# Stores issued behind the loads of the sixth later pair instead of the fourth, in a batched matrix product

## The chip, the cores and the metric

The kernel runs on one core of a Trainium2 chip. The metric is the device time of one execution in microseconds (us). "Span" is the time from the first to the last instruction in a trace; it is about 1.8 us less than the device time of the same execution. Each transfer that uses all 16 DMA engines of the core shows 16 completions in the trace; it has "landed" with the last of them. The engines work through their own queues of transfers ("rings"). "Granted clock" is the share of TensorE's full clock that the profile shows.

## The reference

```python
b1, b2, m, k, n = 8, 16, 256, 512, 384        # 128 products of (256 x 512) by (512 x 384), float32
def reference(x, weight):
    return np.matmul(x, weight).astype(np.float32)
```

## The kernel before

The 128 products are taken in 64 pairs, 0 to 63. For each pair SP (SyncE) issues one load of x (1 MB), two of w (768 KB each) and one store (768 KB). DVE casts to bf16, PE transposes x and multiplies, ACT copies the product out of PSUM, the memory that PE writes to. Each engine has its own program, and they meet at semaphores. The parts that matter (cuts marked):

```python
    AHEAD = 4
    XS, WS, OS = AHEAD, AHEAD * G, 8        # buffers of x, of w, of the product; G = 2
    # ...
    def load(e, n, n0):
        wait(e, x_cast, n - XS + 1)         # the cast of pair n-4 has freed the x buffer
        e.dma_start(x_sb[n0 % XS][:], ...).then_inc(x_in[n0 % XS], 16)
        for i in range(G):
            wait(e, w_cast, n * G + (i + 1 - WS))
            e.dma_start(w_sb[(n0 * G + i) % WS][:], ...).then_inc(w_in[(n0 * G + i) % WS], 16)

    def store(e, n, n0):
        e.wait_ge(o_copied, n * G + G)      # ACT has copied pair n out
        e.dma_start(out=o_rows[...], in_=out_sb[n0 % OS][:]).then_inc(o_out[n0 % OS], 16)
    # ...
    @block.sync
    def _(e):
        U = OS
        for n in range(AHEAD):
            load(e, n, n)
        rounds = (NG - AHEAD) // U
        with e.Fori(0, rounds) as t:
            for s in range(U):
                load(e, t * U + (AHEAD + s), AHEAD + s)
                store(e, t * U + s, s)
        for n in range(rounds * U, NG):
            if n + AHEAD < NG:
                load(e, n + AHEAD, n + AHEAD)
            store(e, n, n)
        # ... then wait for all stores
```

## Time and profile before

| | kernel before |
|---|---|
| device time, median of 3 (range) | 524.96 us (524.79 to 526.66) |
| span of the profiled execution | 524.6 us |
| moved by DMA | 218.12 MB, 414 to 426 GB/s in all of the 40 slices but the first and the last |
| busy share PE, DVE, ACT | 65%, 52%, 39% |

Read it from the transfers: 64 pairs move the same bytes whatever the order, and no compute engine comes near its limit. Only the first and the last of the 40 slices (335 and 238 GB/s) lie far below the steady rate of about 424.

### The profile page before, as it was taken

How to read it: one execution, taken by the hardware profiler on the slowest of the kernel's cores; microseconds unless marked ns; L12 is line 12 of the kernel's file. 1: busy time of each engine (PE TensorE's matmuls, PEld its weight loads, DVE VectorE, ACT ScalarE, POOL GpSimd, SP SyncE). 2: the span in 40 equal slices, each digit the busy share in tenths (PEclk: the TensorE clock that was granted, in tenths of full speed). 3: DMA queues.
4: the chain of work that ended last, by engine and by line, in shares of the span. 5: the costliest groups of instructions: out<-in, count | busy, mean ns of one | idle time of the engine just before them, and what ended most of it. 6: DMA issues, size and time to landing. Idle time of an engine off the chain costs nothing.

```text
span 524.6 us, 5588 instructions
## 1 busy us (share of the span) xinstructions
PE 338.9 (65%) x1536; PEld 191.9 (37%) x1536; DVE 272.4 (52%) x320; ACT 204.3 (39%) x257; POOL 0.7 (0%) x6
## 2 busy tenths in 40 slices
PE   3755676756747576675776656666657666766764
PEld 2533333333333343343333333333334333433331
DVE  4655454464554554645545446455454464554641
ACT  1652424344333343342433434444334334344242
POOL 0000000000000000000000000000000000000000
PEclk9997868688787877878778778787787878778686
DMA  8999999999999999999999999999999999999995
GB/s 335 421 415 414 422 420 424 424 424 421 424 423 423 424 423 424 425 420 425 423 423 424 420 423 426 421 424 425 422 425 422 424 424 422 424 424 422 426 423 238
DMA packets 36868, 218.16 MB, mean 416 GB/s; under 512 B 4096, under 2 KB 4096, under 8 KB 28672
## 3 DMA queue, kind: packets, MB, share of 16 engines
q1 hardware_dynamic: 36864, 218.12, 99.9%
q14 instruction: 3, 0.02, 0.0%
q8 instruction: 1, 0.02, 0.0%
HBM read 167.77 MB, written 50.33 MB: 416 GB/s over the span
## 4 chain that ended last, share of the span: by engine, by line
SPq 73%; DMA 15%; issue 7%; PE 2%; DVE 1%; ACTq 0%; DVEq 0%; ACT 0%
SPq L101 47%; DMA w_sb<-in_weight_dram 15%; SPq L110 14%; SPq L95 10%; PE po L163 2%; SPq L90 1%; DVE x_t L133 1%; DVE w_bf L124 0%; SPq L109 0%; ACTq _compat.py:109 0%; SPq L201 0%; PE pt L151 0%; DVEq L90 0%; DVEq L131 0%; ACT out_sb L180 0%
## 5 line engine op out<-in xcount | busy, mean ns | idle before, releaser
L180 ACT COPY out_sb<-po 64x768 f32<-64x768 f32 x256 | 203.0, 793 | 314.4 <-PE po L163 311.7
L163 PE MATMUL po<-w_bf,x_t 128*128 128x384 bf16 x1024 | 251.9, 419 | 95.3 <-DVE x_t L133 95.3
L163 PEld LDWEIGHTS po<-w_bf,x_t 128*128 128x128 bf16 x1024 | 119.4, 122 | 216.6 <-issue 182.0
L119 DVE CAST x_bf<-x_sb 128x2048 bf16<-128x2048 f32 x64 | 78.5, 1227 | 200.0 <-DMA x_sb<-in_x_dram 200.0
L124 DVE CAST w_bf<-w_sb 128x1536 bf16<-128x1536 f32 x128 | 122.3, 955 | 40.2 <-DMA w_sb<-in_weight_dram 40.2
L151 PE MATMUL pt<-identity,x_bf 128*128 128x128 f32 x512 | 87.7, 322 | 83.8 <-DVE x_bf L119 83.5
L151 PEld LDWEIGHTS pt<-identity,x_bf 128*128 128x128 f32 x512 | 72.5, 211 | 109.1 <-issue 107.9
L133 DVE COPY x_t<-pt 128x1024 bf16<-128x1024 bf16 x128 | 82.2, 683 | 1.1 <-PE pt L151 1.1
L180 ACT ACT_TABLE_LOAD x1 | 1.3, 1283 | 0.9 <-SPq L48 0.9
masks.py:199 POOL TENSOR_SCALAR_AFFINE_SELECT identity<-identity 128x128 f32<-128x128 f32 x1 | 0.3, 293 | 0.2 <-POOL identity L190 0.2
L190 POOL MEMSET identity<- 128x128 f32 x1 | 0.2, 204 | 0.5 <-SPq L48 0.5
L253 POOL MEMSET const-bfloat16-1.0<- 128x1 bf16 x1 | 0.1, 101 | 0.0
L253 POOL MEMSET const-uint8-127<- 128x1 uint8 x1 | 0.1, 101 | 0.0
L253 POOL MEMSET const-float32-0.0<- 128x1 f32 x1 | 0.1, 98 | 0.2 <-issue 0.2
L253 POOL MEMSET const-float32-1.0<- 128x1 f32 x1 | 0.1, 98 | 0.0
## 6 DMA issues: line engine op xcount, KB each, us to landing
w_sb<-in_weight_dram SPq DMA_DIRECT2D x128, 768.0 KB, 22.3
x_sb<-in_x_dram SPq DMA_DIRECT2D x64, 1024.0 KB, 22.6
out_dram<-out_sb SPq DMA_DIRECT2D x64, 768.0 KB, 21.7
```

Of the source, the lines that this page charges most:

```text
L90: e.wait_ge(sem, value)
L95: e.dma_start(x_sb[n0 % XS][:], x_rows[bass.ds(n * (G * M), G * M)].rearrange("(p r) k -> p r k", r=R),).then_inc(x_in[n0 % XS], 16)
L101: e.dma_start(w_sb[(n0 * G + i) % WS][:], w_rows[bass.ds(n * (G * K) + i * K, K)].rearrange("(p ko) n -> p ko n", ko=KO),).then_inc(w_in[( ...
L110: e.dma_start(out=o_rows[bass.ds(n * (G * M), G * M)].rearrange("(p r) n -> p r n", r=R), in_=out_sb[n0 % OS][:],).then_inc(o_out[n0 % OS] ...
L119: e.tensor_copy(out=x_bf[n0 % BS][:], in_=x_sb[n0 % XS][:]).then_inc(x_cast, 1)
L124: e.tensor_copy(out=w_bf[(n0 * G + i) % WBS][:], in_=w_sb[(n0 * G + i) % WS][:]).then_inc(w_cast, 1)
L133: e.tensor_copy(out=x_t[n0 % TS][:, j, :, :, g : g + 2].rearrange("k h i g c e -> k g (h i) (c e)"), in_=pt[(n0 * T + q) % PT][:].bitcast( ...
L151: ins = e.transpose(pt[(n0 * T + q) % PT][:, rr, h, :], words[:, 2 * q + rr, h :: KO // 2], identity[:],)
L163: ins = e.matmul(po[(n0 * G + i) % PO][:, j, :N], x_t[n0 % TS][:, j, ko // 2, i, :, :, ko % 2].rearrange("k g c -> k (g c)"), w_bf[(n0 * G ...
L180: ins = e.copy(out=out_sb[n0 % OS][i * C : (i + 1) * C, g::G, :], in_=po[(n0 * G + i) % PO][g * C : (g + 1) * C, :, :N],)
L190: e.memset(identity[:], 0.0).then_inc(id_done, 1)
L253: nc = _bacc.Bacc("TRN2", target_bir_lowering=False, num_devices=1)
```

## The change

The intent is to let loads run further ahead of stores, so that a store, and the wait that it brings to the issuing queue, never holds a load back, and so that more stores are left to fill the queue while the last pair is computed. All the change is on SP:

```diff
+    LAG = 6
 ...
-        for n in range(AHEAD):
+        for n in range(LAG):
             load(e, n, n)
-        rounds = (NG - AHEAD) // U
+        rounds = (NG - LAG) // U
         with e.Fori(0, rounds) as t:
             for s in range(U):
-                load(e, t * U + (AHEAD + s), AHEAD + s)
+                load(e, t * U + (LAG + s), LAG + s)
                 store(e, t * U + s, s)
         for n in range(rounds * U, NG):
-            if n + AHEAD < NG:
-                load(e, n + AHEAD, n + AHEAD)
+            if n + LAG < NG:
+                load(e, n + LAG, n + LAG)
             store(e, n, n)
```

The buffers stay as they are: four of x, eight of w, eight of the product.

## The prediction

> **What bounds the kernel now.** I read the page first, parts 2 to 4, then the windows of the last microseconds, then the store's line in small windows, then the timeline, then the waits of the issuing queue.
>
> The page, part 2, 40 slices of 13.1 us each:
>
> ```profile
> DMA  8999999999999999999999999999999999999995
> GB/s 335 421 415 414 422 420 424 424 424 421 424 423 423 424 423 424 425 420 425 423 423 424 420 423 426 421 424 425 422 425 422 424 424 422 424 424 422 426 423 238
> ...
> q1 hardware_dynamic: 36864, 218.12, 99.9%
> ```
>
> The transfers bound it. They run at 420 to 426 GB/s in all slices but the first (335) and the last (238), while the busiest compute engine, PE, is at 65%. A change that moves no fewer bytes can only win in those two slices. The first loses its time before any transfer starts (4 GB/s in the window of 0 to 2 us), and every load in it is the same in both kernels. What remains is the last slice. Windows of one microsecond there (columns: window, length, busy us and count of PE, PEld, DVE, ACT, POOL, granted clock, DMA share, GB/s):
>
> ```profile
> 515.00:516.00 1.00, 1.00 (x5) 0.50 (x4) 0.00 (x0) 0.12 (x1) 0.00 (x0) 0.50 1.03 430
> 516.00:517.00 1.00, 1.00 (x5) 0.50 (x4) 0.00 (x0) 0.99 (x2) 0.00 (x0) 0.50 0.77 320
> 517.00:518.00 1.00, 1.00 (x5) 0.32 (x3) 0.00 (x0) 0.48 (x1) 0.00 (x0) 0.76 0.15 61
> 518.00:519.00 1.00, 0.01 (x1) 0.00 (x0) 0.00 (x0) 0.94 (x2) 0.00 (x0) 1.00 0.06 25
> 519.00:520.00 1.00, 0.00 (x0) 0.00 (x0) 0.00 (x0) 0.64 (x1) 0.00 (x0) 1.00 0.03 12
> 520.00:521.00 1.00, 0.00 (x0) 0.00 (x0) 0.00 (x0) 0.00 (x0) 0.00 (x0) 0.95 0.56 233
> 521.00:522.00 1.00, 0.00 (x0) 0.00 (x0) 0.00 (x0) 0.00 (x0) 0.00 (x0) 0.50 1.03 424
> 522.00:523.00 1.00, 0.00 (x0) 0.00 (x0) 0.00 (x0) 0.00 (x0) 0.00 (x0) 0.50 0.33 129
> ```
>
> The hole from about 516.8 to 520.4 is the prize: most DMA engines have nothing to do until the last pair's product is copied out (ACT ends at 519.6) and its store, the only one left, runs from 520.4. But the share in the hole is not zero: 0.15, then 0.06. One sixteenth is 0.0625, so one engine of the 16 is still at work there at its usual rate: a straggler with a backlog.
>
> How late it is, the last five stores tell (answers for the store's line in small windows: start of the issue, and time to landing, which is when the last of the 16 engines is done):
>
> ```profile
> L110 SPq DMA_DIRECT2D out_dram<-out_sb x1: 1609/1609/1609, 492.6 to 492.6; - x1
> DMA to landing us min/median/max: 21.8/21.8/21.8
> L110 SPq DMA_DIRECT2D out_dram<-out_sb x1: 332/332/332, 503.1 to 503.1; - x1
> DMA to landing us min/median/max: 15.1/15.1/15.1
> L110 SPq DMA_DIRECT2D out_dram<-out_sb x1: 332/332/332, 509.8 to 509.8; - x1
> DMA to landing us min/median/max: 10.2/10.2/10.2
> L110 SPq DMA_DIRECT2D out_dram<-out_sb x1: 332/332/332, 519.7 to 519.7; - x1
> DMA to landing us min/median/max: 3.2/3.2/3.2
> ```
>
> Call the pairs 0 to 63. Store 59 lands at 492.6 + 21.8 = 514.4, store 61 at 518.2, store 62 at 520.0, store 63 at 522.9. From 59 to 62 they are (520.0 - 514.4) / 3 = 1.87 us apart: back to back on the slowest engine. Store 63 comes 2.9 us after 62, so this engine had a hole of only 2.9 - 1.87 = 1.0 us. The span ends 1.7 us after that landing (524.6).
>
> The timeline shows the rhythm, by the casts of x, which start when their load lands:
>
> ```profile
> 492.75 1.23 DVE L119 CAST x_bf<-x_sb 128x2048 bf16<-128x2048 f32 x1 [3.21 <-DMA x_sb<-in_x_dram]
> ...
> 500.81 1.23 DVE L119 CAST x_bf<-x_sb 128x2048 bf16<-128x2048 f32 x1 [3.21 <-DMA x_sb<-in_x_dram]
> ...
> 508.89 1.23 DVE L119 CAST x_bf<-x_sb 128x2048 bf16<-128x2048 f32 x1 [3.22 <-DMA x_sb<-in_x_dram]
> ```
>
> 8.07 us per pair, with DVE waiting 3.2 us for each. At the start, with loads alone in the queue, the same casts start at 5.88, 12.12, 18.36 and 24.61: 6.24 us per pair of loads. The difference, 1.83 us, is what one store costs among loads; the 1.87 of stores alone is nearly the same. So mixing loads and stores costs nothing that I can see, and re-ordering them should save nothing in the steady part.
>
> **What the Trainium skill says.** "HBM Reference", Specifications, gives about 425 GB/s for a core that streams alone, bounded by its 16 DMA engines; the trace agrees with 424. "DMA: Bandwidth & Descriptors", Queues, rings and completion order, says that each engine consumes descriptors in ring order and that one transfer is split over up to 16 rings; its section on why a DMA increments by 16 says these engines finish independently. The trace agrees: store 62 lands at 520.0 although total traffic collapses at about 516.8. The same page, Anatomy of one DMA, says semaphore waits happen on the issuing sequencer, not in the DMA engines; so what a load waits for depends on what was issued before it, and the order of issue is all that this diff changes.
>
> **The change, part by part.** No instruction on PE, DVE, ACT or POOL changes; the listing of both kernels differs there by line numbers only. On SP the same 192 loads and 64 stores are issued; six pairs of loads instead of four go before the first store. The buffers stay: four of x, eight of w, so load m still waits for the cast of pair m-4.
>
> 1. Start. Loads 4 and 5 come before store 0. Before, store 0 went out at 17.1 after a wait for ACT, and load 5 only behind it at 17.75. Load 5 can now go when cast 1 is over (13.4). But a transfer lands 22 us after its issue (median), so the queue is deep and stays fed either way. Gain: 0.
>
> 2. Steady part. The queue's own waits are short: the store's wait for ACT is 29.8 us in all, of which 25.6 us lie in the last 40 us, the loads' wait for DVE 10.9 us. SP otherwise stands in the issue instruction itself (1.3 to 5 us each), held by the full queue. So load m goes out about when pair m-3 lands, in both kernels. Moving stores back by two pairs exchanges places in a queue that never empties. Gain: 0. The out buffers have room: store n now goes out as pair n+3 lands and itself lands 22 us, or 2.7 pairs, later; its buffer is wanted for the copy of pair n+8, over 2 pairs after that.
>
> 3. Tail. Load 63 had stores 0 to 58 ahead of it, and now has 0 to 56. Two stores less are 2 x 1.87 = 3.7 us: the last x lands at 505.1 instead of 508.8, and the chain from there to the issue of store 63 (cast, transposes, copies, matmuls, ACT: 519.7 - 508.8 = 10.9 us) ends at about 516.0. That is the gain offered. But behind load 63 now stand six stores (57 to 62) instead of four. The straggling engine has the same bytes to move before store 63 in both kernels, so it is through at 520.0 in both. Store 63 is then already waiting, and lands 1.87 us later, at 521.9, instead of 522.9. Gain: the straggler's hole, 1.0 us, and no more.
>
> Sum: 0 + 0 - 1.0 to -1.1 us, thus 524.96 - 1.1 = 523.9 us, 0.2% less.
>
> **Rivals.** (a) *The full 3.7 us.* If the engines were level, the hole would be 3.5 us for all, and the shift would fill it: 521.3 us. For it: the fifteen other engines. Against it: the 0.06 of DMA share between 518 and 519, and the landing of store 62. A smaller spread in unprofiled runs doesn't open it either: then the last load lands earlier in the old kernel too, and its hole is the same. (b) *No gain.* The last matmuls ran at a granted clock of 0.50 (4.91 us; 2.77 us for an earlier pair at 1.00). In an execution where the clock happens to be full there, the old chain is about 2 us shorter and the old kernel has no hole on the straggler: 525.0 us. For it: the clock alternates all through the run. (c) *Slower, by a wait on the out buffers or by starving compute behind the first six loads.* A wait on the out buffers would need a store to take 40 us instead of 22. Loads alone come every 6.24 us, and DVE needs 272.4 / 64 = 4.3 us per pair, PE 338.9 / 64 = 5.3; at half clock PE needs 1.8 + 4.9 = 6.7, for a few pairs only. I would give it at most 526.
>
> **Range and chances.** Centre 523.9. Below, the full shift with less spread is unlikely, so 522.8. Above, rival (b) and the noise of the runs before (524.79 to 526.66) give 525.3. A change of 2% is 10.5 us; the two end slices together don't hold that much outside the bytes. Faster 0.01, same 0.98, slower 0.01.
>
> **What would show it.** In the new profile: slices 2 to 39 still near 424; the last slice up from 238 to about 285 GB/s (3.76 MB in 13.1 us, if the fifteen run through to about 519.2); the last matmuls starting near 509.4 instead of 513.1; store 63 issued near 516, landing some 6 us later instead of 3.2, and 1.9 us behind store 62; the store's wait for ACT in the tail well under 25.6 us. The prediction is wrong if store 62 lands much before 520 (the straggler depended on the order of transfers), or if the steady rhythm leaves 8.07 us per pair (mixing does cost), or if the first slices lose rate.

## The result, and the profile after

| | before | after |
|---|---|---|
| device time, median (range), 4 runs each | 525.28 us (524.79 to 526.66) | 525.24 us (524.97 to 525.32) |
| span of the profiled execution | 524.6 us | 523.4 us |

The ratio is 0.9994, with a 95% interval of 0.9974 to 1.0014: the same. Ratios here are the mean time of one kernel's fast runs over that of the other's fast runs of the same rounds, so they are not quite the ratios of the medians.

The changed kernel, page part 2, the 40 slices:

```profile
DMA  8999999999999999999999999999999999999996
GB/s 336 421 419 419 426 420 424 424 423 422 423 424 423 422 424 423 423 425 420 424 425 422 424 423 424 424 422 424 425 422 424 424 425 424 422 422 426 423 424 259
```

The first slice (336 for 335) and the steady ones are unchanged, but for the third and the fourth (419 each, for 415 and 414). The last went from 238 to 259. The windows of its end (same columns as in the prediction):

```profile
517.00:518.00 1.00, 0.00 (x0) 0.00 (x0) 0.00 (x0) 0.00 (x0) 0.00 (x0) 0.50 1.01 418
518.00:519.00 1.00, 0.00 (x0) 0.00 (x0) 0.00 (x0) 0.00 (x0) 0.00 (x0) 0.50 0.24 98
519.00:520.00 1.00, 0.00 (x0) 0.00 (x0) 0.00 (x0) 0.00 (x0) 0.00 (x0) 0.50 0.07 31
520.00:521.00 1.00, 0.00 (x0) 0.00 (x0) 0.00 (x0) 0.00 (x0) 0.00 (x0) 0.50 0.06 25
521.00:522.00 1.00, 0.00 (x0) 0.00 (x0) 0.00 (x0) 0.00 (x0) 0.00 (x0) 0.50 0.02 6
```

Before, the hole came ahead of the last store, for most engines. Now there is no hole ahead of it. By the packets of the trace, thirteen engines are done with everything, the last store included, by about 518.4, and two more by 519.5; from then on one engine of the sixteen (a share of 0.06) works alone until 521.3. That all compute is over shows in the five zero columns. Now the chain of the last pair, from the timeline:

```profile
505.12 1.23 DVE L121 CAST x_bf<-x_sb 128x2048 bf16<-128x2048 f32 x1 [3.23 <-DMA x_sb<-in_x_dram]
...
509.32 4.07 PE L165 MATMUL po<-w_bf,x_t 128*128 128x384 bf16 x16 [1.62 <-DVE x_t L135]
512.09 3.22 ACT L182 COPY out_sb<-po 64x768 f32<-64x768 f32 x4 [6.12 <-PE po L165]
```

Its x landed at 505.1 instead of 508.9, 3.8 us earlier. And stores 62 and 63 (the store's line in two small windows):

```profile
L112 SPq DMA_DIRECT2D out_dram<-out_sb x1: 332/332/332, 506.0 to 506.0; - x1
DMA to landing us min/median/max: 13.9/13.9/13.9
L112 SPq DMA_DIRECT2D out_dram<-out_sb x1: 333/333/333, 515.3 to 515.3; - x1
DMA to landing us min/median/max: 6.4/6.4/6.4
```

Store 62 lands at 519.9 (520.0 before). Store 63 is issued 4.4 us earlier than before (515.3 for 519.7), waits in the ring, and lands at 521.7 (522.9 before). So 4.4 us earlier at the issue became 1.2 us at the landing, and the span fell by 1.2 us. Yet the device times say 0.0. That is the question for the experiments, besides whether one engine really takes the 3.2 us in between.

One sign that I had expected is poor. The waits of the issuing queue in the last 40 us, before and then after:

```profile
SPq L110 <- ACT out_sb L180: 25.6, 6, 9.5
```

```profile
SPq L112 <- ACT out_sb L182: 22.0, 4, 9.0
```

SP still waits for ACT almost as long, since it comes to stores 61 to 63 early in both kernels. In the changed kernel this wait costs nothing: the transfers already issued keep the DMA engines busy (a share of 1.00 to 1.01 up to 518).

### The profile page after: what moved, and what is told of

Read it like the earlier page. It is cut to its first block, busy times and chain, and to the rows that moved or that the text cites. A ratio compares the mean times of both kernels' runs of the same rounds, so it can differ in the third digit from the quotient of the medians.

```text
span 523.4 us, 5588 instructions
## 1 busy us (share of the span) xinstructions
PE 330.2 (63%) x1536; PEld 188.7 (36%) x1536; DVE 272.5 (52%) x320; ACT 204.3 (39%) x257; POOL 0.7 (0%) x6
## 4 chain that ended last, share of the span: by engine, by line
DMA 64%; SPq 25%; DVE 4%; issue 3%; PE 1%; ACT 0%; ACTq 0%; DVEq 0%
DMA w_sb<-in_weight_dram 64%; SPq L112 12%; SPq L103 7%; SPq L97 6%; DVE w_bf L126 3%; PE po L165 1%; DVE x_t L135 1%; SPq L92 0%; ACT out_sb L182 0%; ACTq _compat.py:109 0%; SPq L111 0%; DVEq L92 0%; PE pt L153 0%; DVEq L133 0%; SPq L203 0%
## 5 line engine op out<-in xcount | busy, mean ns | idle before, releaser
L165 PE MATMUL po<-w_bf,x_t 128*128 128x384 bf16 x1024 | 243.6, 408 | 95.6 <-DVE x_t L135 95.4
L165 PEld LDWEIGHTS po<-w_bf,x_t 128*128 128x128 bf16 x1024 | 116.6, 119 | 211.6 <-issue 172.7
```

The lines of the kernel that those rows point to most:

```text
L165: ins = e.matmul(po[(n0 * G + i) % PO][:, j, :N], x_t[n0 % TS][:, j, ko // 2, i, :, :, ko % 2].rearrange("k g c -> k (g c)"), w_bf[(n0 * G ...
```

## The experiments

**Theory.** One DMA engine, the straggler, is about 3 us behind the others at the end and never runs dry in the changed kernel; it sets the end. In the kernel before it runs dry in some executions and not in others. **Rival 1**, chain theory: the last pair's compute sets the end in both. **Rival 2**: order does not matter. For the disagreement of spans and times, the theory is that the executions of the kernel before differ, and that its first profile caught a long one.

### The same delay in both kernels: late_after, late_before

To see slack, add to the path and look what comes out at the end. Three more copies of ACT, 2.4 us in all, go ahead of the last pair's signal:

```diff
+        for k in range(3):          # last pair only; into spare buffers
+            ins = e.copy(out=spare[k][i * C : (i + 1) * C, :, :], in_=po[...][...])
         ins.then_inc(o_copied, 1)
```

(ACT's last eight pairs are written out of its loop for it.)

> The changed kernel with three more copies by ACT (0.79 us each, 2.4 us in all, into a spare buffer) ahead of the last pair's signal to store. Straggler theory (the slowest DMA engine is busy without a gap until about 521, whatever ACT does; store 63 waited in the ring behind it): store 63 is issued 2.4 us later, at about 517.9 instead of 515.5, lands in about 4 us instead of 6.4, and the time stays: 0 to +0.3 us against the changed kernel. Chain theory (the last pair's compute sets the end, the rings are level in unprofiled runs): +2.4 us.

> The kernel before with the same three copies. Straggler theory: here store 63 comes when the slowest engine has run dry, so the delay goes to the end: +2.4 us where the hole of 1.0 us of the profile is usual, +1.4 us or so where the usual execution has no hole but about 1 us of slack (which its times, equal to those of the changed kernel, suggest). Chain theory: +2.4 us. Both say it is later than the changed kernel with the delay or equal to it; only the straggler theory says that the two kernels answer differently to the same delay.

Measured in the same rounds: late_after 525.11 us, ratio to before 0.9986 (0.9974 to 0.9998); late_before 527.07 us, ratio 1.0023 (1.0008 to 1.0038). The changed kernel itself, in these rounds too, gave 525.11 us (below). So the delay costs the changed kernel nothing, and the kernel before 1.2 us by the ratio. Store 63 of late_after, then of late_before:

```profile
L113 SPq DMA_DIRECT2D out_dram<-out_sb x1: 333/333/333, 517.7 to 517.7; - x1
DMA to landing us min/median/max: 4.2/4.2/4.2
```

```profile
L111 SPq DMA_DIRECT2D out_dram<-out_sb x1: 332/332/332, 521.5 to 521.5; - x1
DMA to landing us min/median/max: 3.2/3.2/3.2
```

In late_after the issue moved from 515.3 to 517.7 and the landing only from 521.7 to 521.9: the time from issue to landing shrank from 6.4 to 4.2 us and took up the delay. Most engines did run dry there, and it cost nothing, since the latest one was still at work:

```profile
516.00:517.00 1.00, 0.00 (x0) 0.00 (x0) 0.00 (x0) 1.00 (x3) 0.00 (x0) 0.74 0.28 117
517.00:518.00 1.00, 0.00 (x0) 0.00 (x0) 0.00 (x0) 0.66 (x1) 0.00 (x0) 0.50 0.10 43
518.00:519.00 1.00, 0.00 (x0) 0.00 (x0) 0.00 (x0) 0.00 (x0) 0.00 (x0) 0.50 0.55 227
```

In late_before it lands 3.2 us after its issue, the time that it takes with empty rings, and in this execution every delay goes through. The chain theory falls for the changed kernel. That late_before lost less than 2.4 us on average fits a kernel before that has slack in some executions.

### The changed kernel again: after_again, after_3

> The changed kernel again, in the same rounds. Straggler theory with a hole of 1.0 us in the usual execution of before: 1.0 us less than before (0.2%). With no usual hole: equal within 0.1%. The landing of store 63 again some 6 us after its issue.

> The changed kernel again in the same rounds, to compare with: a spread of under 0.8 us, and about 0.6 us (0.1%) under the kernel before on average, since before's slack or hole depends on the granted clock under its last matmuls.

Measured: 525.11 us against 525.79 (ratio 0.9988, 0.9976 to 1.0000) and 525.02 against 525.62 (0.9986, 0.9972 to 1.0000), on two chips. With the runs of the result, that is 15 executions of the changed kernel, 524.62 to 525.45, mean 525.08, and 24 of the kernel before, 524.77 to 526.66, mean 525.63. (The 18 runs of the kernel before in the rounds of other experiments bring its mean to 525.51.) The mean fell by 0.55 us (0.1%), at the edge of what these runs can tell. The spread is plainer: 0.8 us instead of 1.9. The fastest executions of both kernels are alike; the change took away the slow ones. The profile of after_again shows how: its last sixteen matmuls ran at half clock and took 4.89 us, as in the first profile of the kernel before (4.91 us), and yet store 63, issued at 515.5, landed 5.9 us later and the span was 523.1 us, not 524.6.

### More looks at the kernel before: before_2, before_3

The kernel before, unchanged, profiled twice more.

> The kernel before, a second look. Clock theory: what makes its executions differ (spans of 523.0 to 524.9) is the granted clock under the last matmuls, which sets how long the chain from the landing of the last x to the issue of store 63 takes: 10.9 us with half clock, about 9 us with full. A span near 523.0 to 523.5 should show sixteen matmuls at about 2.8 us and store 63 landing no more than 1.9 us behind store 62; a span near 524.5 the 4.9 us of the first profile. Rival (the straggling engine varies instead): equal chains, store 62 landing at different times.

> As before_2, a third look, to have more than one phase of the clock: the span should follow the time of the last sixteen matmuls, 4.9 us with about 524.5, 2.8 us with about 523.

Device times were 525.76 us (span 524.0) and 524.92 us (span 523.1). The last matmuls in the timeline and the last store, of before_2:

```profile
513.01 4.34 PE L163 MATMUL po<-w_bf,x_t 128*128 128x384 bf16 x16 [1.63 <-DVE x_t L133]
```

```profile
L110 SPq DMA_DIRECT2D out_dram<-out_sb x1: 332/332/332, 519.0 to 519.0; - x1
DMA to landing us min/median/max: 3.2/3.2/3.2
```

The same of before_3:

```profile
512.72 2.77 PE L163 MATMUL po<-w_bf,x_t 128*128 128x384 bf16 x16 [1.63 <-DVE x_t L133]
```

```profile
L110 SPq DMA_DIRECT2D out_dram<-out_sb x1: 332/332/332, 517.5 to 517.5; - x1
DMA to landing us min/median/max: 4.0/4.0/4.0
```

With the first profile there are three, and they line up:

| execution of the kernel before | last 16 matmuls start, us | they take, us | store 62 lands | store 63 issued | store 63 lands | span |
|---|---|---|---|---|---|---|
| first profile | 513.1 | 4.9 | 520.0 | 519.7 | 522.9 | 524.6 |
| before_2 | 513.0 | 4.3 | 519.9 | 519.0 | 522.2 | 524.0 |
| before_3 | 512.7 | 2.8 | 519.6 | 517.5 | 521.5 | 523.1 |

Store 62, which only transfers decide, varies by 0.4 us. The matmuls vary by 2.1 us, and the issue of store 63 with them. In before_3 it comes early enough that its landing takes 4.0 us instead of 3.2: it had to wait for the straggler, as in the changed kernel, and the span is even 0.3 us shorter than that kernel's. So, in these three executions, the kernel before has a hole of 1.0 us when the clock is low under its last matmuls, and none when it is full. No experiment set the clock; the three looks are what shows it. "TensorE: Matmul & The Clock Gate", What's actually happening, says that the gate passes half or all of the clock, by activity in windows of about 3.4 us which run freely, not from the kernel's start. The traces agree on the grid: in each of the three, all recorded changes of the clock lie on a grid of 3.41 us, and it stands at another offset from the start of the span in each (2.07, 0.83 and 1.20 us). So the last sixteen matmuls, which started within 0.4 us of each other, met half clock (510.7 to 517.5), part of it (512.8 to 516.2) and full clock (509.8 to 520.0). That activity opens the gate is not tested here.

### Other distances: lag3, lag5

```diff
-    LAG = 6
+    LAG = 3        # and 5 in lag5; lag3 also writes out the first eight rounds of the loop
```

> Stores behind the loads of the third later pair (the first eight rounds of the loop written out, so that no wait is on zero). One store more ahead of load 63 than in the kernel before: the last load lands 1.87 us later, the chain behind it too, and three stores instead of four stand behind it. Straggler theory: the hole on the slowest engine grows by 1.87 us and the time with it, +1.9 us against before (+1.0 or more if before has slack). Rival (order does not matter at all, the end is bytes over rate): 0.

> Stores behind the loads of the fifth later pair. Load 63 lands 1.87 us earlier than in the kernel before, which covers the hole of 1.0 us: store 63 is issued at about 517.8, before the slowest engine is through (518.7 or so). Straggler theory: as the changed kernel, within 0.2 us, and as steady (a spread under 0.8 us). Chain theory: halfway between the two.

| stores behind the loads of the ... later pair | median, us | range, us | ratio to before, same rounds |
|---|---|---|---|
| third (lag3) | 527.54 | 526.78 to 528.77 | 1.0040 (1.0024 to 1.0056) |
| fourth (before) | 525.79 | 524.80 to 526.64 | 1 |
| fifth (lag5; before 525.33 there) | 524.78 | 524.70 to 525.03 | 0.9991 (0.9977 to 1.0004) |
| sixth (after_again) | 525.11 | 524.86 to 525.45 | 0.9988 (0.9976 to 1.0000) |

The first step costs 2.1 us by the ratio (one store of 1.87 us was expected), the later ones next to nothing: rival 2 falls, and the curve goes flat where the straggler takes over. The spread of the times (2.0, 1.8, 0.3, 0.6 us) says the same: only kernels that end on the chain feel the clock. In the profile of lag3 the clock was full (matmuls of 2.77 us), and even so store 63 is issued at 519.7 and lands 3.2 us later, with empty rings:

```profile
L112 SPq DMA_DIRECT2D out_dram<-out_sb x1: 332/332/332, 519.7 to 519.7; - x1
DMA to landing us min/median/max: 3.2/3.2/3.2
```

### Which engine lags: probe

"DMA: Bandwidth & Descriptors", Why a DMA increments its semaphore by 16 and not by 1, says that a transfer that SP issues and whose outer dimension is k, up to 16, uses the lowest-numbered k of the core's engines. So ten tiny loads of 1 to 15 partitions, put behind store 62 in the rings, can show which engine is late:

```diff
+            if n == NG - 1:
+                for k, tile_, sem in zip((1, 2, 4, 6, 8, 10, 12, 13, 14, 15), spot, seen):
+                    e.dma_start(tile_[:k, :], x_rows[0:k, 0:P]).then_inc(sem, 16)
             store(e, n, n)
```

> The changed kernel with ten very small loads between the issues of stores 62 and 63, spread over the first 1, 2, 4, 6, 8, 10, 12, 13, 14 and 15 DMA engines (as many partitions each). They stand in the rings behind store 62, so each lands when the latest of its engines is through store 62. Straggler theory: up to some number they land with the level engines, at about 517, from that number on with the straggler, at about 520: the step names the engine; if none steps, it is the last one. Rival (no fixed engine, the spread is of each transfer): no step, a slow rise. Time within 0.3 us of the changed kernel.

The last completion of each, read from the trace, in us from the span's start:

| engines used | 1 | 2 | 4 | 6 | 8 | 10 | 15 |
|---|---|---|---|---|---|---|---|
| landed at | 516.1 | 516.8 | 517.8 | 520.0 | 520.2 | 520.4 | 521.2 |

Each probe adds some 0.2 us to the one behind it, and the first four engines lie up to 1.3 us apart (the four completions of the third probe come at 516.5, 517.0, 517.3 and 517.9); between four engines and six the step is 2.2 us, and of the two engines that come in there the other is level (its completion comes at 516.4). Store 62 itself landed at 519.8 on its last engine and at 516.7 on the median one. So in this execution the straggler is, by that rule, the fifth or the sixth engine, and it is one engine, though the others are not quite level either. The trace agrees with the rule as to how many: each probe showed as many completions as it has partitions, and one more right after its issue. The trace has no numbers of engines. (The time, one look, was 525.78 us, 0.7 us over the changed kernel where 0.3 us was expected: a miss.)

### Where its lag comes from: pe_pairs2

The completions of every trace show the engines level within 0.5 us for the first ten or so transfers. Then one engine falls 1.3 to 1.8 us behind the median one, within some microseconds of the only instruction packet of 16 KB (queue 8 in part 3 of the page; at 32.2 us, about 1.1 us long, in the changed kernel). After that the largest lag drifts up slowly, to 3.2 us at store 62 there. The test was to halve PE's program, the longest:

```diff
     @block.tensor
-        U = 4
+        U = 2
```

> The changed kernel with PE's program in a loop of two pairs behind two written out, instead of four behind four: half of its instructions. In all ten profiles so far one engine falls 1.2 us behind the others just after the single instruction packet of 16 KB (queue 8, about 1 us long, at 32 to 45 us), and stays behind. If that packet fetches PE's program, it is gone or shorter here, store 62 lands at about 518.8 instead of 520.0, and the time is 1.0 to 1.2 us under the changed kernel's (about 524.0). Rival (the packet is another engine's, or the drift alone makes the straggler): no change, 525.1.

Measured 524.97 us (ratio 0.9989, 0.9976 to 1.0003) beside 525.02 for the changed kernel. The packet was still there, at 45.0 us, and store 62 landed at 519.8. The packet is not PE's, or doesn't depend on the length of PE's program; whose it is stays open.

The traces show more, which the test passed over. The first fall follows the packet: over the fourteen traces it starts anywhere from 32.1 to 45.0 us, and in each the first transfer with an engine over 0.8 us late lands 2.0 to 4.1 us after it. But that engine is not the one that is late at the end. In five traces (before, before_3, after, after_3, lag5) nearly every packet can be given to its engine, since each starts within some nanoseconds of the end of the one before. There the engine that the packet met keeps its lag or makes some of it good (in the changed kernel from 1.5 to 1.2 us), and another overtakes it, at about 160 us in the changed kernel. This one's 8 KB packets, the loads of x, take 312.0 to 313.3 ns on average between 60 and 480 us, where those of every other engine in the same traces take 309.0 to 311.1; that is the drift. This suggests that a kernel without the packet would keep its straggler; no run shows it. Why those packets take longer stays open.

### Less work for the straggler: off_first4, off_first8

Stores 61 and 62 are cut so that the straggler moves two packets less, or two more:

```diff
-            store(e, n, n)
+            (store_split if n in (NG - 3, NG - 2) else store)(e, n, n)
# store_split: one transfer of 112 partitions, then 16 partitions in transfers of W = 4 (or 8)
```

> The changed kernel with stores 61 and 62 cut: 112 partitions as before over all sixteen engines (seven packets of 6 KB for each instead of eight), the other 16 partitions in four transfers of four partitions, which go to the first four engines alone (the probe: those are level ones, the straggler is the fifth or sixth). The straggler moves two packets less (0.234 us each): if it alone sets the end, 0.5 us less than the changed kernel, about 524.6, and up to 1 us less than the other kernel of this call. Rival (all engines together, or the last pair's chain, set the end): no less, or more by the issue of eight more transfers.

> The same cut, with the 16 partitions in two transfers of eight, which go to the first eight engines, the straggler among them: per store it moves seven packets and two, one more than before. Straggler theory: 0.5 us more than the changed kernel, about 525.5. Rival: the same time as off_first4, or less, since it issues four transfers fewer.

Measured 527.71 us (ratio 1.0047) and 528.39 us (1.0062), both slower by far more than the packets in question. By its letter off_first4 failed the straggler theory, and "no less, or more" was the rival's forecast. Windows of off_first4 show why the test can't be used:

```profile
514.00:515.00 1.00, 0.00 (x0) 0.00 (x0) 0.00 (x0) 0.26 (x1) 0.00 (x0) 0.97 0.97 356
515.00:516.00 1.00, 0.00 (x0) 0.00 (x0) 0.00 (x0) 0.00 (x0) 0.00 (x0) 0.50 0.93 344
516.00:517.00 1.00, 0.00 (x0) 0.00 (x0) 0.00 (x0) 0.00 (x0) 0.00 (x0) 0.50 1.00 363
```

The engines are as busy as ever (0.93 to 1.00) and move 344 to 363 GB/s where the changed kernel moves 418. In the trace single packets of 6 KB take up to 1.43 us, where all take 0.23 to 0.26 in the last 13 us of the changed kernel. The packets became slower with the cut. The order of the two kernels is the one expected (off_first8 is 0.7 us later), but under such a disturbance it shows nothing. I don't know which part of the cut does it.

## Why the prediction was right or wrong

The measured 525.24 us lies in the range, near its upper end, and "same" was right. That says little, since any change under 10.5 us would have been "same": of the gain of 1.1 us the medians show 0.04. By the steps of the prediction:

- **Start, 0: held** on the latest engine. The first slice is 336 GB/s for 335, and store 62 lands at the same time.
- **Steady part, 0: held.** The casts of x in the tail are 8.08 us apart (497.04 to 505.12), and the steady slices are at 419 to 426. Mixing loads and stores shows no price here. Three readings were loose: of the "last five stores" four are shown (store 60 landed at 516.2), the kernel before had 415 and 414 GB/s in its third and fourth slices, not 420 to 426 in all but two, and about half of the issues of x loads took 0.33 us, not 1.3 to 5.
- **Tail, the chain: held.** Last x foreseen at 505.1, cast at 505.12; last matmuls foreseen at 509.4, begun at 509.32; store 63 foreseen at 516.0, issued at 515.3, since the clock was full for part of its matmuls.
- **Tail, the straggler: held.** Store 63 foreseen at 521.9, landed at 521.7; the span 523.4 against 523.5 (524.6 - 1.1). late_after shows that the ring, not the chain, then sets the end. The last slice was foreseen at 285 GB/s and came to 259, since thirteen of the other fifteen engines were through at 518.4, not all at 519.2: the median engine had landed store 62 at 516.7, 0.7 us earlier than before. That the fifteen are level was too simple: at store 62 the second latest is 1.0 us behind the median before, and 1.2 after. That changes nothing at the end.
- **Sum: the step that failed.** "Thus 524.96 - 1.1 = 523.9" subtracts a gain that was measured in one execution from the median of others. The profiled execution of the kernel before took 526.41 us, not 524.96: with half clock under its last matmuls it was a long one, and the hole of 1.0 us belongs to such executions. The median of three was an execution near the floor already. Carried through on one scale, the step would have read 523.5 + 1.8 = 525.3 us. The term called "the straggler's hole" is 1.0 us at half clock and zero at full (before_3), and 0.55 us on the mean of 24 runs and 15.
- **Rivals.** (a), the full 3.7 us (521.3 us), fell with the result, and its level engines with late_after. (b), no gain when the clock is full at the end, is what before_3 shows; I gave it too little weight, as a matter of noise in the upper end of the range. (c), slower, did not happen.

## What to carry to other kernels

When transfers bound a kernel, ask at its end which single DMA engine is through last, not when the total rate falls: here only a gap on that engine could be closed, and a share of one sixteenth in a window betrayed it. A deeper order of loads before stores paid here until the last store reached the rings before that engine was free (lag5); what it brought up to there was mostly steadiness, by hiding the chain's dependence on the clock. And compare a change with the execution that was profiled: add its own time, not the median of others.

## What the Trainium skill lacked or had wrong

- "DMA: Bandwidth & Descriptors", Latency and other measured facts, names engines 7 and 15 as usually slower, and that for transfers issued by GpSimd. Here, with SP issuing all, one engine was late by 2.4 to 3.5 us against the median one at store 62 in the profiles of all kernels with uncut stores; in the one probed it was, by the page's own rule, the fifth or sixth (number 4 or 5 from 0). No page has an engine whose 8 KB packets take longer than the others' (312.0 to 313.3 ns against 309.0 to 311.1).
- The same page has no word on how deep the queue of an issuing sequencer is before the issue itself stands still. Here a transfer lands 22 us after its issue at four transfers per 8.07 us, so about eleven are in flight (an estimate from these two), and in the steady part the issue instructions take 0.3 to 4.9 us each.
- No page gives the price of mixing directions in one queue. Here a store costs 1.83 us among loads and 1.87 among stores: none that these runs show.
- The same page states how many engines a transfer of few partitions uses, but not what a cut of a 128-partition store does to the rest: 112 partitions and some small transfers brought packets from 0.23 us up to 1.43 us.
